# One bank for the first half's pooled maps, a first pair of merge gates and an earlier place for reloaded keys in an fp32 hybrid layer on one core

## The chip, the cores and the metric

The kernel runs as one program on one core of a Trainium2 chip. TensorE multiplies, VectorE (DVE in the profile), ScalarE (ACT) and GpSimd (POOL) do the rest, and SyncE (SP) starts most of the transfers. The metric is the time of one execution on the device in microseconds, the median of several.

## What is computed

One layer with two token mixers is applied to 2048 prompt rows and to 64 sample rows that continue a cached sequence of 4096 positions. All values are fp32.

```
h = rmsnorm(x);  q,k,v,ga,u,gb,mg = split(h @ w_in)        # 1024 columns each, mg 2048
att = stick_breaking(q, k, v)                              # 8 heads of 128; sample rows also see cache_k, cache_v
   A[t,s] = sigmoid(z_ts) * prod_{s<j<t} (1 - sigmoid(z_tj)),  s < t
pb  = (trailing_mean(u, 2|4|8|16) - u) per group of 256 columns, @ w_pool[group], * pool_scale
y_a = (att * silu(ga)) @ w_br_a;   y_b = (pb * silu(gb)) @ w_br_b
x   = x + (sigmoid(mg)[:, :1024] * y_a + sigmoid(mg)[:, 1024:] * y_b) @ w_out
return rmsnorm(x), k, v and the last 15 rows of u, for prompt and sample
```

## The kernel before

**Products.** Each fp32 operand is split into a high and a low part of reduced width (hi and lo in the names), and each product of 128 x 128 weights with up to 512 columns is three matmuls: hi with hi, lo with hi, hi with lo. A cast on ScalarE makes the high part and a subtraction on VectorE the low one; the function `split` issues both, and in the profile they appear in the lines of that helper (L91, L92, and L341 where program order is kept). So `wlo<-raw,whi` is the low part of a weight slab, `klo<-kback,khi` that of a block of keys that was read back from memory.

**Stages.** The rows are handled in two halves: the first has 1088 columns (1024 prompt rows and the 64 sample rows, in groups of 512, 256 and 320 in the profile), the second 1024. The stages follow each other in time, in us of the profiled execution:

- up to about 575: projections and attention of the first half, head by head;
- 575 to 1085: attention of the sample rows over the cache (`sample_stream`), with the first half's gates and its four pool groups (`rest`) between its steps;
- 1090 to 1790: projections and attention of the second half, some 93 us per head;
- 1795 to 1880: the attention left over from the last head, beside the branch gates (columns of `gb`) 0 to 3;
- 1880 to 2230: the second half's pool groups, branch gates 4 to 7 and the merge gates (the sixteen 128-column slabs of `mg`);
- then the branch products `w_br_a` and `w_br_b`, the merge, `w_out` (in steps n = 0 to 7) and the last norm.

**Order.** TensorE's instructions stand in the order in which the code issues them, over the whole program; `run((a, cost), (b, cost))` interleaves two generators by the nanoseconds that they yield. On ScalarE, VectorE and SyncE a scheduler sets the order in most of the program; inside `manual_schedule` blocks and in `placed_split` it is the code's order.

**Accumulators.** The eight PSUM banks are dealt out by name, two to each: `pj` for projections, `tr` for transposes and scans' tails, `att` for attention's output, `z` for scores. The sample attention keeps one `att` bank as its accumulator through a pair of heads.

**Pool groups.** `pool_group(half, gi)` projects two slabs of `u`, forms the trailing means and, in `mapped`, multiplies them with the 256 x 256 weights of the group: for each column group (g, of n columns), two products (s = 0 and 1, called A and B here), each of six matmuls into a PSUM tile, and then one multiplication on VectorE (L502, `gbl<-z,pscale,gbl`) that reads the tile and scales it with the gate. In the first half there are four groups with three column groups each, so 12 pairs A, B. In the groups of 512 columns the twelve matmuls of A and B stand back to back on TensorE; in those of 256 and 320 six projection matmuls stand between A and B.

**Second half's heads.** `Attention.scores(n)` is called for each of the 28 units of a head. Blocks of the first half's keys and values are read back from memory (`kback`, `vback`) and split at units that are set by a key: block cc of k at unit 5 - 2 cc, of v at 9 - 2 cc. A head's own late block of v (`late_v`, from the tile `nat`) is split at unit 1.

**Gates.** A slab of gates is eight chunks of weights times two groups of 512 columns, 48 matmuls (`proj`, lines 368 to 370). `proj_ahead` is `proj` with weights whose loads and splits were issued ahead by hooks in the attention units, from the list `cols_ahead`. Branch gates 6 and 7 (`branch_pair`) and merge gates 2 to 15 (`GATE_PAIRS`) are made two slabs at a time in seven products of 12 matmuls each, by a scheme of sums: the row sums of h (`hs["a11"]`, `hs["s1"]` and so on) are made once (`form_sums`), the sums of the weight blocks for each pair (`pair_forms`). Merge gates 0 and 1 are plain slabs of 48.

**The last stages.** `load_rows` fetches row blocks for the branch products, `weight_sums` forms the sums of `w_br` and `w_out` beside the merge gates, and `norm_sums` takes squares of the output rows on ScalarE (`bjk<-xo`, L1817) for the last norm.

## Time and profile before

| | |
|---|---|
| three runs | 2685.87, 2688.13, 2689.59 us; median 2688.13 |
| the profiled execution | 2687.25 us, of which the span of the core's instructions is 2685.5 |
| TensorE | busy 2663.5 us, 99% of the span, 15078 matmuls |
| VectorE | 1910.3 us, 71% |
| ScalarE | 1321.2 us, 49% |
| GpSimd | 418.4 us, 16% |
| memory | 341.40 MB moved by the queues, mean 127 GB/s |

A row of the timeline gives the start of an instruction in us after the start of the span, its duration, engine, line, operation, what it writes and reads, shapes, and in brackets how long its engine had been idle and what ended that. "x2" is two instructions in a row. The duration of a matmul contains its way through the array, so matmuls overlap: the pace is the distance of two starts. In the view of waits, a row gives the engine and line that waited, what ended the wait, the total in us, how often, and the longest.

### The profile page before, as it was taken

What the parts mean: (1) busy time and instruction counts of PE and PEld (TensorE: products, weight loads), DVE (VectorE), ACT (ScalarE), POOL (GpSimd) and SP (SyncE); (2) the same over time, 40 slices, a digit from 0 to 9 for tenths busy, and PEclk for the clock granted to TensorE, in tenths of its full rate; (3) what the DMA queues carried; (4) which work ended last, traced back from release to release, by engine and by line L of the source; (5) the groups of instructions that cost most, each with busy time, mean ns of one, the idle gap of its engine ahead of it and who ended that gap; (6) DMA issues with size and microseconds to landing.
All of it is one profiled execution on the core that took longest, in us unless ns stands there. A gap on an engine that the chain in (4) does not pass through costs nothing.

```text
span 2685.5 us, 42349 instructions
## 1 busy us (share of the span) xinstructions
PE 2663.5 (99%) x15078; PEld 2347.1 (87%) x15078; DVE 1910.3 (71%) x3016; ACT 1321.2 (49%) x2621; POOL 418.4 (16%) x1202
## 2 busy tenths in 40 slices
PE   9999999999999999999999999999999999999998
PEld 8999899988899989988888888888888889999886
DVE  6555555567777784488888888888956757677877
ACT  5446444455555553365556656655432443332443
POOL 1122222220000000021222222121001301111001
PEclk9999999999999999999999999999999999999999
DMA  5224222234444444222111111111345868787753
GB/s 152 82 82 131 75 74 74 80 100 151 154 150 154 153 151 159 83 59 59 44 48 57 58 36 60 56 40 48 118 134 169 281 204 290 234 283 252 257 176 118
DMA packets 336594, 341.40 MB, mean 127 GB/s; under 512 B 29736, under 2 KB 278944, under 8 KB 336383
## 3 DMA queue, kind: packets, MB, share of 16 engines
q1 hardware_dynamic: 322270, 292.82, 34.7%
q0 software_dynamic: 14112, 45.89, 4.7%
q8 instruction: 118, 1.93, 0.3%
q14 instruction: 94, 0.76, 0.1%
HBM read 229.97 MB, written 108.65 MB: 126 GB/s over the span
## 4 chain that ended last, share of the span: by engine, by line
PE 92%; DVE 5%; issue 1%; ACT 1%; POOL 1%; DMA 0%; DVEq 0%; POOLq 0%; SPq 0%; ACTq 0%
PE pj L368 15%; PE pj L369 15%; PE pj L370 15%; PE tr L819 4%; PE x L1528 3%; PE x L1532 3%; PE x L1530 3%; PE y L1532 3%; PE y L1528 3%; PE y L1530 2%; PE att L836 2%; PE att L835 2%; PE z L807 2%; PE att L834 2%; PE z L806 2%; PE z L805 2%
## 5 line engine op out<-in xcount | busy, mean ns | idle before, releaser
L368 PE MATMUL pj<-hhi,whi 128*128 128x512 f32 (+2 forms) x2320 | 830.2, 358 | 0.0
L370 PE MATMUL pj<-hhi,wlo 128*128 128x512 f32 (+2 forms) x2320 | 803.7, 346 | 0.0
L369 PE MATMUL pj<-hlo,whi 128*128 128x512 f32 (+2 forms) x2320 | 803.2, 346 | 0.3 <-DVE hlo L1072 0.3
L743 DVE TENSOR_TENSOR_SCAN om<-om 128x513 f32<-128x513 f32 (+3 forms) x356 | 387.0, 1087 | 193.4 <-POOL om L720 103.2
L370 PEld LDWEIGHTS pj<-hhi,wlo 128*128 128x128 f32 x2320 | 437.1, 188 | 52.0
L368 PEld LDWEIGHTS pj<-hhi,whi 128*128 128x128 f32 x2320 | 438.6, 189 | 46.9
L369 PEld LDWEIGHTS pj<-hlo,whi 128*128 128x128 f32 x2320 | 438.4, 189 | 45.3 <-DVE hlo L1072 0.5
L735 ACT ACTIVATE om<-z 128x512 f32<-128x512 f32 (+2 forms) x320 | 170.9, 534 | 291.1 <-PE z L807 270.1
L746 DVE TENSOR_TENSOR be<-be,om 128x512 f32<-128x512 f32 (+3 forms) x356 | 218.8, 614 | 33.4 <-ACT a L91 0.5
L92 DVE TENSOR_TENSOR a<-tr,a 128x512 fp32r<-128x512 f32 (+2 forms) x356 | 216.0, 607 | 28.2 <-ACT a L91 25.9
L91 ACT CAST a<-tr 128x512 fp32r<-128x512 f32 (+2 forms) x356 | 188.1, 528 | 86.5 <-PE tr L819 78.7
L745 POOL COPY carry<-om 128x1 f32<-128x1 f32 x356 | 71.6, 201 | 858.0 <-DVE om L743 832.0
L819 PE MATMUL tr<-ident,be 128*128 128x128 f32 x1088 | 173.9, 273 | 5.5 <-DVE be L746 4.4
L819 PEld LDWEIGHTS tr<-ident,be 128*128 128x128 f32 x1088 | 135.9, 140 | 38.9 <-DVE be L746 8.0
L736 ACT ACTIVATE be<-z 128x512 f32<-128x512 f32 (+2 forms) x320 | 169.5, 530 | 0.0
L92 DVE TENSOR_TENSOR wlo<-raw,whi 128x512 fp32r<-128x512 f32 x157 | 107.3, 688 | 84.5 <-ACT whi L91 83.9
L91 ACT CAST whi<-raw 128x512 fp32r<-128x512 f32 x160 | 98.7, 622 | 87.8 <-PE pj L369 76.6
L834 PE MATMUL att<-a,v 128*128 128x512 f32 (+1 forms) x320 | 132.7, 415 | 0.0
L836 PE MATMUL att<-a,v 128*128 128x512 f32 (+1 forms) x320 | 118.4, 370 | 1.8 <-DVE a L92 1.5
L807 PE MATMUL z<-khi,qlo 128*128 128x512 f32 (+2 forms) x320 | 117.0, 365 | 0.0
L835 PE MATMUL att<-a,v 128*128 128x512 f32 (+1 forms) x320 | 116.5, 364 | 0.0
L806 PE MATMUL z<-klo,qhi 128*128 128x512 f32 (+2 forms) x320 | 116.4, 364 | 0.0
(496 smaller groups left out, 5209.8 us busy)
## 6 DMA issues: line engine op xcount, KB each, us to landing
raw<-in_w_in_dram SPq DMA_DIRECT2D x228, 256.0 KB, 2.9
sg<-sm_d SPq DMA_DIRECT2D x48, 352.0 KB, 5.4
kraw<-in_cache_k_dram SPq DMA_DIRECT2D x64, 256.0 KB, 3.2
vraw<-in_cache_v_dram SPq DMA_DIRECT2D x64, 256.0 KB, 2.9
sm_d<-sgm SPq DMA_DIRECT2D x48, 256.0 KB, 3.0
wraw<-tw_d SPq DMA_DIRECT2D x22, 512.0 KB, 4.0
out_dram<-nat SPq DMA_DIRECT2D x42, 256.0 KB, 2.3
mp_d<-sg POOLq DMA_DIRECT2D x24, 352.0 KB, 5.1
```

The source lines that it names most:

```text
L91: nc.scalar.copy(hi, src)
L92: (nc.gpsimd if eng == "g" else nc.vector).tensor_tensor(lo, src, hi.bitcast(F32), op=ALU.subtract)
L368: nc.tensor.matmul(ps[:, 0:n], whi[:, k], hhi[:, k, c0:c0 + n], start=k == 0, stop=False)
L369: nc.tensor.matmul(ps[:, 0:n], whi[:, k], hlo[:, k, c0:c0 + n], start=False, stop=False)
L370: nc.tensor.matmul(ps[:, 0:n], wlo[:, k], hhi[:, k, c0:c0 + n], start=False, stop=k == KT - 1)
L735: nc.scalar.activation(om[:, off:512], z[:, off:512], AF.Sigmoid, scale=-SCALE)
L743: nc.vector.tensor_tensor_scan(rev, rev, rev, 1.0, op0=ALU.mult, op1=ALU.bypass)
L746: nc.vector.tensor_tensor(be[:, off:512], be[:, off:512], om[:, off + 1:513], op=ALU.mult)
L807: nc.tensor.matmul(z[:, off:512], qlo[:, qs], khi[:, 0:m], start=False, stop=True)
L819: nc.tensor.transpose(tr[:, i * P:(i + 1) * P], be[:, off + j * P:off + (j + 1) * P], ident)
L834: nc.tensor.matmul(self.acc[:, s], vhi[:, js], ahi[:, s], start=first, stop=False)
L836: nc.tensor.matmul(self.acc[:, s], vhi[:, js], alo[:, s], start=False, stop=last)
```

## The change

It has six parts.

1. In the first half, the pooled maps' PSUM tile is named `att` and not `z`. The order of TensorE's instructions stays as it was there.
2. In the second half's heads, reloaded blocks of keys are split at unit 3 - 2 cc, so cc = 1 at unit 1 and cc = 0 at unit 3; a late block of v at unit 2.
3. Branch gates 0 to 3 are no longer in `cols_ahead` and go through `proj`.
4. Merge gates 0 and 1 become a pair (`stream_forms`, `first_gates`) in seven products of 12 matmuls, behind the last pool group. Their weight sums and the first four of the pair 2, 3 (11 forms) are made by `stream_forms`, `pair_forms` makes the other three of that pair, and `weight_sums` takes its steps later.
5. Of `load_rows`, the blocks r12 and r22 are both fetched at step (5, 0).
6. `norm_sums(0)` of step n = 0 of `w_out` moves from the end of that step into step 1.

The order on TensorE at the first pooled maps of 512 columns, before and after (buffer numbers kept; a name with another number is another tile; "waits" names the engine whose semaphore is waited for). Rows of before:

```order
L500 MATMUL z_7660<-phi_7520,wplo_7343 128x512
L498 MATMUL z_7669<-phi_7428,wphi_7342 128x512
L499 MATMUL z_7669<-plo_7429,wphi_7342 128x512
L500 MATMUL z_7669<-phi_7428,wplo_7343 128x512
L498 MATMUL z_7669<-phi_7520,wphi_7342 128x512
L499 MATMUL z_7669<-plo_7521,wphi_7342 128x512
L500 MATMUL z_7669<-phi_7520,wplo_7343 128x512
L919 MATMUL z_7683<-khi_7451,q2_7106 128x512 [waits DVE_49]
```

The same place on TensorE now:

```order
L500 MATMUL att_7660<-phi_7520,wplo_7343 128x512
L498 MATMUL att_7669<-phi_7428,wphi_7342 128x512 [waits DVE_49]
L499 MATMUL att_7669<-plo_7429,wphi_7342 128x512
L500 MATMUL att_7669<-phi_7428,wplo_7343 128x512
L498 MATMUL att_7669<-phi_7520,wphi_7342 128x512
L499 MATMUL att_7669<-plo_7521,wphi_7342 128x512
L500 MATMUL att_7669<-phi_7520,wplo_7343 128x512
L918 MATMUL z_7683<-khi_7451,q2_7106 128x512
```

Nothing changed its place. The first matmul of B (tile 7669) now waits for VectorE, and the score product behind it no longer does: since the other `att` bank holds the sample attention's accumulator, A and B have the same bank.

On TensorE within the first merge gates, into which the last maps of the last pool group fall (`z<-phi`, set off behind their projections). Rows of before, where `pj<-hhi` is merge gate 0 as a plain slab:

```order
L498 MATMUL z<-phi,wphi 128x512
L499 MATMUL z<-plo,wphi 128x512
L500 MATMUL z<-phi,wplo 128x512
L368 MATMUL pj<-hhi,whi 128x512
L369 MATMUL pj<-hlo,whi 128x512
L370 MATMUL pj<-hhi,wlo 128x512
L368 MATMUL pj<-hhi,whi 128x512
L369 MATMUL pj<-hlo,whi 128x512
L370 MATMUL pj<-hhi,wlo 128x512
L514 MATMUL tr<-ident,hist 15x128 x2
L368 MATMUL pj<-hhi,whi 128x512
```

The same place now:

```order
L498 MATMUL z<-phi,wphi 128x512
L499 MATMUL z<-plo,wphi 128x512
L500 MATMUL z<-phi,wplo 128x512
L514 MATMUL tr<-ident,hist 15x128 x2
L1230 MATMUL pj<-s3hi,whi 128x512
L1231 MATMUL pj<-s3lo,whi 128x512
L1232 MATMUL pj<-s3hi,wlo 128x512
L1230 MATMUL pj<-s3hi,whi 128x512
```

Products with sums of h (`s3`) stand where plain slabs stood, and the list of TensorE's rows is 12 shorter (13498 for 13510); it differs nowhere else but in the names of part 1 and in line numbers.

On VectorE in the first units of the second half's second head (`om`, `be` and `a` are a unit's scan, weights and their low part). Rows of before:

```order
L341 TENSOR_TENSOR v<-nat,v 128x512
L743 SCALAR_TENSOR_TENSOR om<-om 128x257
L746 TENSOR_TENSOR be<-be,om 128x256
L92 TENSOR_TENSOR a<-tr,a 128x512
L341 TENSOR_TENSOR wlo<-raw,whi 128x512
L743 SCALAR_TENSOR_TENSOR om<-om 128x385
L746 TENSOR_TENSOR be<-be,om 128x384
L92 TENSOR_TENSOR a<-tr,a 128x512
L89 CAST khi<-kst 128x512
L92 TENSOR_TENSOR klo<-kst,khi 128x512
L341 TENSOR_TENSOR klo<-kback,khi 128x512
L743 SCALAR_TENSOR_TENSOR om<-om 128x513
```

The same place now, from one unit's start on:

```order
L341 TENSOR_TENSOR klo<-kback,khi 128x512
L742 SCALAR_TENSOR_TENSOR om<-om 128x257
L745 TENSOR_TENSOR be<-be,om 128x256
L92 TENSOR_TENSOR a<-tr,a 128x512
L341 TENSOR_TENSOR wlo<-raw,whi 128x512
L341 TENSOR_TENSOR v<-nat,v 128x512
L742 SCALAR_TENSOR_TENSOR om<-om 128x385
L745 TENSOR_TENSOR be<-be,om 128x384
L92 TENSOR_TENSOR a<-tr,a 128x512
L89 CAST khi<-kst 128x512
L92 TENSOR_TENSOR klo<-kst,khi 128x512
L341 TENSOR_TENSOR klo<-kback,khi 128x512
```

The block cc = 1 has moved up two units, to the front; the block cc = 0 has taken its place behind `klo<-kst`; and v stands one unit later, beside a weight's low part.

The diff, its core:

```
                 c = gi * 2 + s
-                pb = psum.tile([P, 512], F32, name="z")
+                pb = psum.tile([P, 512], F32, name="z" if half else "att")
                 co = slice(s * P, (s + 1) * P)
...
                     if late_v:
-                        placed.setdefault(hd, []).append((1, out["v"], c0h + c, vchunk, nat))
+                        placed.setdefault(hd, []).append((2, out["v"], c0h + c, vchunk, nat))
                     else:
...
                     cols_ahead.extend(o + h * P for h in range(1, H) for o in (OFF_K, OFF_V, OFF_Q, OFF_GA))
-                    cols_ahead.extend(OFF_GB + c * P for c in range(4))
             else:
...
                         nc.sync.dma_start(raw, kvd[kind, hd, cc])
-                        todo.append(({"k": 5, "v": 9}[kind] - 2 * cc, out[kind], cc, chunk, raw))
+                        todo.append(({"k": 3, "v": 9}[kind] - 2 * cc, out[kind], cc, chunk, raw))
                 todo.sort(key=lambda x: x[0])
...
         pns = slab_ns(1)
-        run((tail_att, tail_ns), (chain(*[proj_ahead(GROUPS_B, branch_gate(1, c)) for c in range(4)]), 4 * pns))
+        run((tail_att, tail_ns), (chain(*[proj(GROUPS_B, [branch_gate(1, c)]) for c in range(4)]), 4 * pns))
         settle(True)
...
+        def stream_forms(c0):
+            half = []
+            def put(src):
+                if not half:
+                    t = form_w()
+                    half.extend([x[:, 4 * h:4 * h + 4] for x in t] for h in range(2))
+                w = half.pop(0)
+                split(*w, src)
+                ready.append(w)
+            def part_raw(nm):
+                return late[0].tile([P, 512], F32, name=nm).rearrange("p (k c) -> p k c", k=4)
+            for c in (c0, c0 + 2):
+                b = {nm: raw_w(OFF_M + (c + j) * P, k) for nm, j, k in (("b11", 0, 0), ("b12", 1, 0), ("b21", 0, 4))}
+                b["b22"] = part_raw("r12")
+                col = OFF_M + (c + 1) * P
+                nc.sync.dma_start(b["b22"], win[:, col:col + P].rearrange("(k p) c -> p k c", p=P)[:, 4:8, :])
+                if c == c0:
+                    yield
+                put(b["b11"])
+                yield
+                put(b["b21"])
+                yield
+                t2 = part_raw("r11")
+                nc.vector.tensor_tensor(b["b11"], b["b12"], b["b11"], op=ALU.subtract)
+                nc.vector.tensor_tensor(t2, b["b22"], b["b11"], op=ALU.subtract)
+                put(t2)
+                yield
+                put(b["b11"])
+                yield
+                if c == c0:
+                    nc.vector.tensor_tensor(b["b12"], b["b22"], b["b12"], op=ALU.subtract)
+                    put(b["b12"])
+                    yield
+                    put(b["b22"])
+                    yield
+                    nc.vector.tensor_tensor(b["b21"], b["b21"], t2, op=ALU.subtract)
+                    put(b["b21"])
+        ready = []
+        def first_gates(c, prepare):
+            next(prepare)
+            next(prepare)
+            x = psum.tile([P, 512], F32, name="pj")
+            kept_x = {}
+            for p, nm in enumerate(("a11", "a12", "s2", "s1", "s3", "s4", "a22")):
+                if p in (1, 3):
+                    y = psum.tile([P, 512], F32, name="att")
+                acc = x if p in (0, 2, 4, 6) else y
+                gate_product(acc, ready.pop(0), hs[nm], p in (0, 1, 3))
+                if p in (0, 2, 3):
+                    kept_x[p] = late[0].tile([P, 512], F32, name=("r21", "r22", None, "r21")[p if p != 2 else 1])
+                    nc.scalar.copy(kept_x[p], acc)
+                elif p < 6:
+                    gate_sum(c + (p != 1), p == 4, acc, kept_x.pop({1: 0, 4: 3, 5: 2}[p]))
+                else:
+                    last_gate.append(lambda: gate_out(c, 1, acc))
+                for _ in range({1: 2, 3: 1, 5: 2}.get(p, 0)):
+                    next(prepare)
+                yield 12 * mm_ns(512)
+        last_gate = []
         def lead(prepare):
...
         run((pool_group(1, 2), 2 * pns), (lead(prepare), 1.0))
-        run((chain(branch_pair(6, prepare), pool_group(1, 3), proj(GROUPS_B, [merge_gate(1, 0)])), 1.0))
+        run((chain(branch_pair(6, prepare), pool_group(1, 3)), 1.0))
+        prepare = stream_forms(0)
+        next(prepare)
+        next(prepare)
+        next(prepare)
+        run((first_gates(0, prepare), 1.0))
         settle(True)
...
                 (b11, b12), (b21, b22) = [[t[:, :, j * P:(j + 1) * P] for j in range(2)] for t in raws.pop(c)]
-                yield pair_form(b11)
-                yield pair_form(b21)
+                kept_forms = c > GATE_PAIRS[0]
+                if kept_forms:
+                    yield pair_form(b11)
+                    yield pair_form(b21)
                 t2 = gw.tile([P, 4, P], F32, name="gt2")
                 nc.vector.tensor_tensor(t2, b22, b11, op=ALU.subtract)
-                yield pair_form(t2)
-                yield pair_form(b11)
+                if kept_forms:
+                    yield pair_form(t2)
+                    yield pair_form(b11)
                 nc.vector.tensor_tensor(b12, b22, b12, op=ALU.subtract)
...
         pair_loads(GATE_PAIRS[0])
+        last_gate.pop()()
         forms_of = pair_forms()
-        ready = []
-
-        def some_forms():
-            for _ in range(4):
-                yield 1.0
-                ready.append(next(forms_of))
-
-        run((chain(*[proj(GROUPS_B, [merge_gate(1, c)]) for c in range(1, GATE_PAIRS[0])]), 10.0), (some_forms(), 8.0))
         closing_sums = weight_sums()
...
                         gate_sum(c + (p != 1), p == 4, acc, kept_x.pop({1: 0, 4: 3, 5: 2}[p]))
+                    if c == GATE_PAIRS[0]:
+                        next(prepare, None)
                     w = next(forms_of, None)
                         ready.append(w)
-                    next(closing_sums, None)
+                    if c > GATE_PAIRS[0] or p > 2:
+                        next(closing_sums, None)
                     if c + 2 == GATE_PAIRS[1]:
...
                 weights_at(2 * s + cc)
-                if more and (p, cc) in ((2, 0), (3, 0), (5, 0), (5, 1)):
-                    load_rows(s + 7 - p, {2: "r11", 3: "r21", 5: ("r12", "r22")[cc]}[p])
+                if more and (p, cc) in ((2, 0), (3, 0), (5, 0)):
+                    for nm in {2: ("r11",), 3: ("r21",), 5: ("r12", "r22")}[p]:
+                        load_rows(s + 7 - p, nm)
                 if not more and (p, cc) == (5, 1):
...
             elif not last:
+                if n == 1:
+                    norm_sums(0)
                 norm_sums(1)
...
             product(x, of.pop((n, "a22")), wo["t4"], False, cols, whole)
-            if not last:
+            if n and not last:
                 norm_sums(0)
```

## The prediction

> **What bounds the kernel now.** I read the page first, its busy times, the granted clock and the chain that ended last:
>
> ```profile
> PE 2663.5 (99%) x15078; PEld 2347.1 (87%) x15078; DVE 1910.3 (71%) x3016; ACT 1321.2 (49%) x2621; POOL 418.4 (16%) x1202
> PEclk9999999999999999999999999999999999999999
> PE 92%; DVE 5%; issue 1%; ACT 1%; POOL 1%; DMA 0%; DVEq 0%; POOLq 0%; SPq 0%; ACTq 0%
> ```
>
> TensorE is busy for 99% of the span at full clock and carries 92% of the chain. So the time is the number of matmuls times their pace, plus the moments in which TensorE waits. Only two kinds of edit can move it: matmuls added or removed, and waits of TensorE made or ended. The second view is therefore the waits of TensorE over the whole span (its largest rows), the third the busy time by stretches of the stages that the change touches:
>
> ```profile
> PE tr L819 <- DVE be L746: 4.4, 10, 1.2
> PE z L919 <- DVE gbl L502: 1.9, 4, 0.7
> PE att L836 <- DVE a L92: 1.5, 3, 0.9
> ...
> 1795.00:1885.00 90.00, 87.32 (x437) 70.78 (x436) 74.87 (x101) 50.59 (x99) 18.34 (x58) 1.00 0.16 55
> 1885.00:2060.00 175.00, 175.00 (x778) 144.59 (x777) 123.39 (x221) 57.28 (x103) 4.46 (x8) 1.00 0.40 128
> ```
>
> There is little to win: four waits of 1.9 us in all are owed to the pooled maps' banks (L502 frees them), the tail of the second half's attention (1795 to 1885) holds 90 − 87.32 = 2.68 us of idle TensorE, and the gates behind it hold none. Last, the timeline at the places that the change touches. The pace of matmuls, and the cost of a wait:
>
> ```profile
> 626.12 0.40 PE L499 MATMUL z<-plo,wphi 128*128 128x512 f32 x1
> 626.36 0.40 PE L500 MATMUL z<-phi,wplo 128*128 128x512 f32 x1
> 627.28 0.40 PE L498 MATMUL z<-phi,wphi 128*128 128x512 f32 x1
> 627.48 0.75 DVE L502 SCALAR_TENSOR_TENSOR gbl<-z,pscale,gbl 128x512 f32<-128x512 f32 x1 [0.20 <-PE z L500]
> 628.87 0.75 DVE L502 SCALAR_TENSOR_TENSOR gbl<-z,pscale,gbl 128x512 f32<-128x512 f32 x1 [0.64 <-PE z L500]
> 629.68 0.50 PE L919 MATMUL z<-khi,q 128*128 128x512 f32 x1 [0.38 <-DVE gbl L502]
> ```
>
> From 626.12 to 627.28 are five starts, (627.28 − 626.12)/5 = 0.23 us each. A matmul's 0.40 reaches 0.17 past the next possible start, so an idle time in brackets understates the loss by 0.17. The score product at 629.68 starts 0.06 after the end of the scaling that it waited for (628.87 + 0.75 = 629.62): that is the price of a release.
>
> **The maps in one bank (part 1).** No instruction comes or goes. At 627.28 the product B starts without a wait while VectorE only begins to scale A (627.48). In the changed order B's first matmul waits for that scaling. So each of the 12 pairs costs the end of A's scaling, plus 0.06, less B's start of before, where this is positive. The other three pairs of 512 columns, B's start and then A's scaling:
>
> ```profile
> 746.07 0.39 PE L498 MATMUL z<-phi,wphi 128*128 128x512 f32 x1
> 747.22 1.41 DVE L502 SCALAR_TENSOR_TENSOR gbl<-z,pscale,gbl 128x512 f32<-128x512 f32 x2
> 864.78 0.40 PE L498 MATMUL z<-phi,wphi 128*128 128x512 f32 x1
> 866.32 0.74 DVE L502 SCALAR_TENSOR_TENSOR gbl<-z,pscale,gbl 128x512 f32<-128x512 f32 x1
> 982.50 0.40 PE L498 MATMUL z<-phi,wphi 128*128 128x512 f32 x1
> 983.84 0.75 DVE L502 SCALAR_TENSOR_TENSOR gbl<-z,pscale,gbl 128x512 f32<-128x512 f32 x1
> ```
>
> The first pair gives 628.23 + 0.06 − 627.28 = 1.01; with 0.75 for one scaling the others give 1.96, 2.34 and 2.15, because VectorE is behind with the sample attention there: 7.5 us. In the pairs of 256 and 320 columns six projection matmuls stand between A and B and cover part of it. Of the four pairs of 256 the first and the last, and the one pair of 320 in which the scaling is late:
>
> ```profile
> 635.80 0.28 PE L498 MATMUL z<-phi,wphi 128*128 128x256 f32 x1
> 637.20 0.48 DVE L502 SCALAR_TENSOR_TENSOR gbl<-z,pscale,gbl 128x256 f32<-128x256 f32 x1
> 992.25 0.28 PE L498 MATMUL z<-phi,wphi 128*128 128x256 f32 x1
> 992.81 0.48 DVE L502 SCALAR_TENSOR_TENSOR gbl<-z,pscale,gbl 128x256 f32<-128x256 f32 x1
> 888.88 0.31 PE L498 MATMUL z<-phi,wphi 128*128 128x320 f32 x1
> 889.38 0.55 DVE L502 SCALAR_TENSOR_TENSOR gbl<-z,pscale,gbl 128x320 f32<-128x320 f32 x1
> ```
>
> They give 1.94 and 1.10, the two between them, read the same way, about 0.5 and 2.2: 5.7. The pair of 320 gives 889.93 + 0.06 − 888.88 = 1.1, the other three nothing. Gross: 7.5 + 5.7 + 1.1 = 14.3 us. Against it the four waits of the scores for a z bank end, 1.9 + 4 × 0.17 = 2.6. Net **+11.7**. Behind the waiting matmul stand the rest of B, then a score product, whose result ScalarE copies for VectorE; those get it later by the same time, but they follow TensorE and catch up while it stands. Low end: VectorE is free each time, every pair of 512 costs the first one's 1.01, the others nothing, 4.0 − 2.6 = +1.4. High end: the waits for a bank come back elsewhere, and one operation more of VectorE, as long as the longest shown below (1.75), falls in front of a scaling: 14.3 + 1.8 = +16.1. I take the middle value since the order on VectorE ahead of each first scaling is the old one.
>
> **The pair of merge gates (part 4).** 7 × 12 = 84 matmuls for 2 × 48 = 96: 12 × 0.23 = **−2.8**. The forms take the places of the weights' splits on VectorE, which has room there; first row, the low part of merge gate 0, second, the next form after both gates, before which VectorE lay idle for 10.76 us:
>
> ```profile
> 2022.98 0.69 DVE L92 TENSOR_TENSOR wlo<-raw,whi 128x512 fp32r<-128x512 f32 x1 [0.16 <-ACT whi L91]
> 2054.46 0.69 DVE L92 TENSOR_TENSOR flo<-graw,fhi 128x512 fp32r<-128x512 f32 x1 [10.76 <-ACT fhi L91]
> ```
>
> Eleven forms and their differences are some 17 operations of 0.69, 12 us over the pair's 20: hidden. Without that cover, a form that waits for its weights would stop TensorE for the length of a transfer and a split; I bound that by 3 us. Ends −2.8 and +0.2.
>
> **Keys and values at other units (part 2).** The waits in the second half's heads are one per head; the first, the second and the last:
>
> ```profile
> 1154.29 0.30 PE L819 MATMUL tr<-ident,be 128*128 128x128 f32 x1 [0.78 <-DVE a L92]
> 1238.40 0.33 PE L819 MATMUL tr<-ident,be 128*128 128x128 f32 x1 [0.47 <-DVE be L746]
> 1704.88 0.33 PE L819 MATMUL tr<-ident,be 128*128 128x128 f32 x1 [0.44 <-DVE be L746]
> ```
>
> The first goes (0.78 + 0.17). The six of later heads stay: they follow the jam of `klo<-kst` and `klo<-kback`, and the block cc = 0 now lands where cc = 1 stood. New is v beside a weight's low part one unit earlier, 0.69 more on VectorE in one unit. I take **−0.6**; ends −4.5 (all seven gone, 0.95 + 6 × 0.6) and +2 (0.3 in each head).
>
> **The tail of attention, and plain branch gates (parts 2 and 3).** Its waits, and what VectorE and GpSimd do just before:
>
> ```profile
> 1799.46 1.59 DVE L341 TENSOR_TENSOR klo<-kback,khi 128x512 fp32r<-128x512 f32 x1
> 1799.22 1.29 POOL L840 TENSOR_TENSOR ao<-ao,sga 128x512 f32<-128x512 f32 x1
> 1804.12 0.44 PE L836 MATMUL att<-a,v 128*128 128x384 f32 x1 [0.29 <-DVE a L92]
> 1809.37 0.33 PE L819 MATMUL tr<-ident,be 128*128 128x128 f32 x1 [1.24 <-DVE be L746]
> 1851.11 1.75 DVE L341 TENSOR_TENSOR wlo<-raw,whi 128x512 fp32r<-128x512 f32 x1
> 1855.66 0.44 PE L836 MATMUL att<-a,v 128*128 128x384 f32 x1 [0.94 <-DVE a L92]
> ```
>
> The two subtractions take 1.59 and 1.75 where their like take 0.69 (rows above), the first beside GpSimd's product, and each is followed by waits. Now the keys' one comes four units sooner, and the weights' low parts of the branch gates are made by `proj`, which feeds branch gates 4 and 5 behind with no idle TensorE (175.00 of 175 above). All of it is 2.68 + 4 × 0.17 = 3.4; some subtractions stay in the tail, so I take two thirds, **−2.3**, ends −3.4 and 0. The Trainium skill, page "SBUF — State Buffer", section "Who interferes with whom", says that a VectorE instruction with two SBUF inputs contends with a GpSimd instruction that reads SBUF; the trace agrees here (1.59 against 0.69), and by that rule alone the term would be the two stretches, 0.90 + 1.06 = 2.0.
>
> **The rest (parts 5 and 6).** The squares of step n = 0 stand ahead of the copy of x on ScalarE, for which TensorE waits once:
>
> ```profile
> 2539.00 0.50 PE L1528 MATMUL x<-t2hi,rhi 128*128 128x512 f32 x1 [0.59 <-ACT x L1543]
> ```
>
> In step 1 they stand behind such a copy: 0.59 + 0.17 = **−0.8**, ends −0.8 and +0.8 (they delay the next copy). Row loads and later weight sums cost nothing: VectorE's 10.76 us of idle and the gates between them and the branch products hide them; without these they would stop TensorE for a transfer, as a late form would (3 us).
>
> **Sum.** +11.7 − 2.8 − 0.6 − 2.3 − 0.8 = **+5.2 us**. The profiled execution took 2687.25, which gives 2692.4; the median of the runs is 0.88 higher, and on it the sum is 2693.3, +0.19%. What a measurement can tell from no change is about 0.2%, 5.4 us (2682.7 to 2693.5), so the forecast lies at that edge.
>
> **Rivals.** (a) VectorE is free when the first maps end, and the one bank costs only its low end: 1.4 − 6.5 = −5.1, 2683.0, faster from a little better on. For it speaks the first pair, where VectorE idled 0.20 us before the scaling; against it the pairs at 635, 746, 864 and 982, in which the scaling began 1.15 to 1.54 us after B's old start. The place to look is the six waits at 635, 746, 864, 877, 982 and 992; it decides where they sum to less than 5 us. (b) The waits pile up: the scores' bank waits come back and the gains of the tail and the keys stay out, 5.2 + 2.6 + 2.9 = +10.7, 2698.8. For it speaks that VectorE is also late elsewhere (the 4.4 us of the first waits row), against it that the removed waits have no other cause in the order. (c) The pair's forms come late by 3 us at its first or third product: 2696.3. (d) The maps don't share a bank and part 1 only removes the waits: −2.6 − 6.5 = −9.1, 2679.0; the wait in the changed order speaks against it. (e) The nine new stalls slow the clock: half pace for 12 matmuls after each is 9 × 12 × 0.23 = 25 us, 2718. Against it, the granted clock is 1.00 in the stretch from 1795 to 1885 with its 2.68 us of waits. The Trainium skill, page "TensorE: Matmul & The Clock Gate", section "A second HAM failure mode: psum-queue depth-cycling", tells of a kernel in which short idle times between groups of matmuls let the clock swing to half; the rows here do not show that for stalls up to 1.24 us.
>
> **How the numbers follow.** The sum as it stands has 0.62; its own range is 2689 to 2697 (the bank's net by ±3, the other terms by ±2), 0.36 within 0.2% and 0.26 above. (a) 0.13, half faster and half the same; (b) 0.15, slower; (c) 0.06, mostly slower; (d) 0.03, faster; (e) 0.01. Faster 0.10, same 0.44, slower 0.46. The range from 2685 to 2699 takes in the sum's own range, (b), (c) and the upper part of (a).
>
> **What would show it.** Right: waits of TensorE for L502 at the maps of about 14 us, half of it at the four pairs of 512 columns, no wait of the scores for L502, 12 matmuls fewer with no wait from 2030 to 2055, the waits near 1809 and 1855 gone, the one at 2539 gone, those near 1238 to 1705 still there. Wrong: VectorE's scaling of A begins right behind A's last matmul (then the time falls to the left end), or waits of over 0.3 us in the heads' second unit or at the pair (right end).

## The result, and the profile after

The changed kernel takes 2708.57 us (median of four runs, 2708.32 to 2711.49) beside 2687.73 us of the kernel before (its median over four runs): the ratio is 1.0077, with an interval from 1.0065 to 1.0090. It is slower by 20.8 us where 5.2 were forecast, and outside the range. Of all runs told below two took far longer, 5359.67 us (the kernel before, beside e1 to e4) and 7021.77 us (e9); they count in the medians and not in the ratios. The profiled execution of the changed kernel has a span of 2706.5 us against 2685.5. Of the page the span and the row of the engines:

```profile
span 2706.5 us, 42389 instructions
PE 2670.0 (99%) x15066; PEld 2350.8 (87%) x15066; DVE 1916.2 (71%) x3028; ACT 1327.7 (49%) x2627; POOL 419.0 (15%) x1202
```

TensorE has 12 matmuls fewer (15066 for 15078) and is nevertheless busy for 6.5 us longer: part of the loss is not waiting but slower matmuls. The largest rows of its waits over the span:

```profile
PE att L498 <- DVE gbl L502: 12.9, 9, 2.2
PE tr L818 <- DVE be L745: 6.4, 11, 1.5
PE z L1230 <- ACT gx L1419: 3.0, 1, 3.0
...
PE y L1600 <- DVE rlo L92: 0.6, 1, 0.6
PE att L1230 <- ACT whi L91: 0.5, 1, 0.5
```

The first row is the one bank of the maps: nine waits, as read from before. The third and the fifth of the rows shown are new and were not forecast: they lie at the first pair that the kernel before made in seven products too, merge gates 2 and 3. The waits of the scores for L502 and the wait at 2539 are gone. Since the order on TensorE is known, the same matmul can be found in both traces, and the difference of its starts shows where the time went:

| stretch of before, us | shift gained there, us | what it is made of |
|---|---|---|
| 0 to 575 | −0.2 | |
| 575 to 1085, maps and sample attention | +15.4 | nine waits +14.4, four ended −2.6, slow matmuls +3.2, slower starts after releases +0.4 |
| 1085 to 1795, heads | +0.5 | first head −0.6, the others +1.1 |
| 1795 to 1885, tail | −0.2 | |
| 2031 to 2058, merge gates 0 and 1 | −2.7 | 12 matmuls |
| 2058 to 2070, merge gates 2 and 3 | +5.7 | waits 0.6 and 3.2, restarts 0.3, slow matmuls 1.6 |
| 2200 to 2225, first branch products | +0.9 | a wait for `rlo` |
| 2225 to 2537, branch products and w_out | +2.0 | pace of the 352-column matmuls |
| 2537 to 2685 | −0.3 | −0.9 at the old wait, +0.6 after it |

The slow matmuls are seen in the busy time by stretches (TensorE's busy time and matmuls, the granted clock, then the transfers). Four stretches of 3.4 us, each right behind a wait, of 2.18, 2.35, 2.02 and 3.16 us from start to start:

```profile
638.00:641.40 3.40, 3.23 (x17) 0.63 0.71 220
874.00:877.40 3.40, 3.40 (x14) 0.56 0.26 98
889.50:892.90 3.40, 3.37 (x22) 1.00 0.49 154
2083.20:2086.60 3.40, 3.40 (x9) 0.56 0.82 255
```

Behind three of the four the granted clock is 0.56 to 0.63 of full over the 3.4 us, and in the last nine matmuls stand where 15 fit at 0.23 us. This is the half clock that the prediction had put at 1 in 100.

The waits at merge gates 2 and 3, in rows picked from the timeline of ScalarE, with the two matmuls of TensorE that waited and GpSimd's issue of the weight sums' loads (`ws`) among them:

```profile
2071.07 0.59 ACT L1419 COPY gx<-z 128x512 f32<-128x512 f32 x1 [2.11 <-PE z L1232]
2071.07 2.35 POOL L1429 DMA_DIRECT2D ws<-in_w_br_a_dram  x4 [171.77 <-PE z L1232]
2076.24 0.62 ACT L91 CAST whi<-raw 128x512 fp32r<-128x512 f32 x1 [4.58 <-PE z L1231]
2076.91 0.50 PE L1230 MATMUL att<-s1hi,whi 128*128 128x512 f32 x1 [0.48 <-ACT whi L91]
2079.55 0.62 ACT L91 CAST fhi<-graw 128x512 fp32r<-128x512 f32 x1 [2.69 <-DVE graw L1411]
2081.53 0.63 ACT L1222 ACTIVATE sgm<-gx 128x512 f32<-128x512 f32 x1 [1.36 <-DVE gx L1235]
2082.57 0.58 ACT L1419 COPY gx<-z 128x512 f32<-128x512 f32 x1
2083.20 0.80 PE L1230 MATMUL z<-s3hi,fhi 128*128 128x512 f32 x1 [3.00 <-ACT gx L1419]
```

The eleventh form's cast (2076.24) stands on ScalarE behind the copy of the first product, but starts only when TensorE has finished the third product, 4.58 us later: it waits for a weight buffer. TensorE's fourth product needs this form (0.48). Behind the cast stand, in order, the next forms and the copy of the third product (2082.57), and the fifth product writes into the bank that this copy frees: 3.00 us. The loads of the weight sums, issued at 2071.07, use buffers of the same two tags as the forms, and had taken the one that the first product freed.

### The profile page after: what moved, and what is told of

Same layout as the page of the kernel before. It is cut to its first block, busy times and chain, and to the rows that moved or that the text cites. A ratio compares the mean times of both kernels' runs of the same rounds, so it can differ in the third digit from the quotient of the medians.

```text
span 2706.5 us, 42389 instructions
## 1 busy us (share of the span) xinstructions
PE 2670.0 (99%) x15066; PEld 2350.8 (87%) x15066; DVE 1916.2 (71%) x3028; ACT 1327.7 (49%) x2627; POOL 419.0 (15%) x1202
## 3 DMA queue, kind: packets, MB, share of 16 engines
q8 instruction: 118, 1.93, 0.3%
## 4 chain that ended last, share of the span: by engine, by line
PE 87%; DVE 7%; issue 3%; ACT 1%; DMA 1%; POOL 1%; POOLq 0%; SPq 0%; DVEq 0%; ACTq 0%
PE pj L368 14%; PE pj L369 14%; PE pj L370 14%; PE tr L818 4%; PE x L1598 3%; PE x L1602 3%; PE x L1600 3%; PE y L1602 2%; PE y L1600 2%; PE y L1598 2%; DVE om L742 2%; PE att L835 2%; PE z L806 2%; PE att L834 2%; PE z L805 2%
## 5 line engine op out<-in xcount | busy, mean ns | idle before, releaser
L368 PE MATMUL pj<-hhi,whi 128*128 128x256 f32 (+2 forms) x2288 | 818.3, 358 | 0.0
L369 PE MATMUL pj<-hlo,whi 128*128 128x256 f32 (+2 forms) x2288 | 791.5, 346 | 0.3 <-DVE hlo L1071 0.3
L370 PE MATMUL pj<-hhi,wlo 128*128 128x256 f32 (+2 forms) x2288 | 791.8, 346 | 0.0
L92 DVE TENSOR_TENSOR wlo<-raw,whi 128x512 fp32r<-128x512 f32 x169 | 115.6, 688 | 98.6 <-ACT whi L91 98.0
L91 ACT CAST whi<-raw 128x512 fp32r<-128x512 f32 x172 | 106.4, 622 | 99.0 <-PE pj L369 77.0
```

Source lines behind the costliest of these rows:

```text
L91: nc.scalar.copy(hi, src)
L92: (nc.gpsimd if eng == "g" else nc.vector).tensor_tensor(lo, src, hi.bitcast(F32), op=ALU.subtract)
L368: nc.tensor.matmul(ps[:, 0:n], whi[:, k], hhi[:, k, c0:c0 + n], start=k == 0, stop=False)
L369: nc.tensor.matmul(ps[:, 0:n], whi[:, k], hlo[:, k, c0:c0 + n], start=False, stop=False)
L370: nc.tensor.matmul(ps[:, 0:n], wlo[:, k], hhi[:, k, c0:c0 + n], start=False, stop=k == KT - 1)
```

## Experiments

All of these leave the computation whole. Their ratios are to runs of the kernel before on the same chip, whose medians were 2688.94 (e1 to e4), 2687.72 (e5 to e7) and 2688.07 us (e8, e9).

**The change without its first part (e1), and the first part alone (e2).**

```
 e1, in the changed kernel           e2, in the kernel before
-name="z" if half else "att"        -name="z"
+name="z"                           +name="z" if half else "att"
```

> The changed kernel with its first part undone: the first half's maps are in the z banks again, all else as changed. Theory: the stretch from 575 to 1085 us gave 15.5 of the 21 us (11.8 of net waits for the scaling, 3.7 of matmuls at half clock behind two of them), so the time falls by about 15.5 to 2693, the four waits of the scores come back, and no stretch near 640 or 875 has a granted clock below 0.95. Rival: the slow matmuls near 640 and 875 belong to the place (weights or transfers there), not to the stalls: then the fall is 11.8, to 2697, and they stay slow.

> The kernel before with the first part alone (maps in the att banks). Theory: +15.5 us, about 2703, with nine waits of 14.4 us together for the scaling and at least one stretch at half clock behind a wait of over 2 us. Rival, the waits alone cost: +11.8, about 2699.5.

e1 took 2689.23 us, ratio 1.0003 (0.9994 to 1.0013); e2 2703.04 us, ratio 1.0056 (1.0041 to 1.0071). So most of the loss is the first part, and without it the rest of the change is worth nothing in sum. The times do not simply add up: the first part costs 14.1 us alone and 20.5 on top of the rest (20.8 against 0.3). The traces differ there by falls of the clock (one more near 638 and one at the merge gates, some 1.5 us each) and by the pace of the last stage, but one trace of each kernel cannot say how often either comes. The stretch from 575 to 1085 is −15.5 us in e1 beside the changed kernel, as expected, with the scores' four waits back (first row); 0.4 of it is lost again before 575. Two things were not expected: the wait of 3.0 us at merge gates 2 and 3 is there in e1 too, but this time without a fall of the clock (rows two and three), which is 1.3 us less there, and the last stage runs 2.0 us faster. With 0.5 less at the first branch products the spans differ by 18.8 and not 15.5.

```profile
PE z L918 <- DVE gbl L502: 1.9, 4, 0.7
...
2068.12 0.50 PE L1230 MATMUL z<-s3hi,fhi 128*128 128x512 f32 x1 [3.00 <-ACT gx L1419]
2068.10:2071.50 3.40, 3.38 (x15) 1.00 0.74 227
```

In e2 the nine waits are the same, but only one of the two waits that were followed by slow matmuls in the changed kernel is so here:

```profile
PE att L498 <- DVE gbl L502: 12.8, 9, 2.2
...
638.70:642.10 3.40, 3.36 (x24) 1.00 0.67 210
872.50:875.90 3.40, 3.40 (x14) 0.69 0.20 77
```

The same instruction with the same wait (2.18 us) was followed by half clock in one execution and by full clock in the other. It is therefore not the place alone. The runs of e2 spread from 2700.3 to 2705.9.

**What decides on the clock (p1, p2).** Ahead of the second half's pool groups of the kernel before stand 60 batches of matmuls with a stall of known length between them; nothing else is changed. The edit in short, not word for word:

```
+ for i in range(60):
+     for j in range(n):  matmul(ps, wt if j == 0 else hhi[:, j % 8, 0:P], hhi[:, j % 8, 512:1024], ...)
+     tensor_tensor(t2, ps, t); further operations of VectorE on t2, about 0.3*(i % 12) us   # p2: 0.55 + 0.1*(i % 10)
+     wt = t2[:, 0:P] - t2[:, 0:P]          # the next batch's first weights
```

> The kernel before with a probe ahead of the second half's pool groups: 60 batches of 52 to 82 matmuls of 512 columns, and behind each a chain of VectorE operations on which the next batch's first matmul depends, so that TensorE stands for about 0.9 to 4.2 us in twelve steps of 0.3, five of each at different distances. Only the trace counts. Theory (the clock falls when TensorE has been idle for the larger part of some window of time whose position is not tied to the kernel): no slow matmuls behind stalls below 1.5 us, in some cases behind those of 2 to 3, in all behind those over 3.5, at half pace for a fixed time of some 3.4 us, 1.7 us lost each. Rival (the slow matmuls depend on what is stalled, the maps or the gates): full pace behind all of them.

> The same probe with stalls between about 1.5 and 2.8 us in ten steps of some 0.1, six of each, behind batches of other lengths. Only the trace counts. In the first probe none of ten stalls up to 1.72 us was followed by slow matmuls, one of five at 1.98, four of five at 2.44 and all five at 2.70. Theory (a window of time not tied to the kernel decides): the share of stalls with slow matmuls rises step by step from none near 1.8 to all near 2.6, with both outcomes at one and the same length. Rival (a fixed length of idle time decides): one length below which none and above which all are followed by them.

In p1 none of the ten stalls up to 1.72 us (from start to start, less the pace) was followed by slow matmuls, one of five at 1.98, four of five at 2.44, all ten at 2.70 and 3.16, four of five at 3.42, and all 24 above 3.8. In p2 both outcomes came at every length from 1.94 to 3.12 but 3.03 and a single stall of 2.04, and the share did not rise steadily: two of five at 1.94, five of six at 2.49, one of six at 2.66, all six at 3.03, one of five at 3.12. Two stalls of one length from p1, each with the stretch behind it, and two from p2:

```profile
2408.46 0.50 PE L1193 MATMUL z<-hhi,pw 128*128 128x512 f32 x1 [1.83 <-DVE pw L1202]
2408.50:2411.50 3.00, 3.00 (x13) 1.00 0.00 0
2884.44 0.50 PE L1193 MATMUL z<-hhi,pw 128*128 128x512 f32 x1 [1.83 <-DVE pw L1202]
2884.50:2887.50 3.00, 3.00 (x9) 0.64 0.00 0
```

```profile
2595.43 0.50 PE L1193 MATMUL z<-hhi,pw 128*128 128x512 f32 x1 [2.96 <-DVE pw L1202]
2595.50:2598.50 3.00, 3.00 (x13) 1.00 0.00 0
2397.87 0.50 PE L1193 MATMUL z<-hhi,pw 128*128 128x512 f32 x1 [2.96 <-DVE pw L1202]
2397.90:2400.90 3.00, 3.00 (x10) 0.73 0.02 5
```

A fixed length of idle time does not decide. What fits is a window: if time is cut into pieces of 3.413 us with one starting point for each execution, "more than some 1.9 us idle within one piece" tells the stalls with slow matmuls from those without, for all 59 stalls of p1 and all 59 of p2. (The length was looked for from 1.6 to 1.8 and from 3.38 to 3.44 us.)

That fit is a calculation on the rows, but the granted clock in the traces shows the pieces themselves. All 43 falls of p1 and all 33 of p2 are stretches at half clock of 3.41 us or of twice that, and within one execution their starts lie on a grid of 3.413 us, to within 0.001 us. With this grid in place of a fitted starting point (its pieces ended 0.1 us before the recorded falls, which fits best) 116 of the 118 stalls come out right at 1.93 us. The three falls of the changed kernel, at 638.91, 874.43 and 2082.75, lie 69 and then 354 such pieces apart. The first, with the piece before it and the piece behind it:

```profile
635.49:638.91 3.42, 1.40 (x11) 1.00 0.27 79
638.91:642.32 3.41, 3.41 (x16) 0.50 0.48 154
642.32:645.73 3.41, 3.41 (x18) 1.00 0.67 210
```

This also answers for the two waits that were followed by half clock in one execution and not in the other. The wait of 2.18 us near 638 lies in one piece in the changed kernel; in e2 the grid of its one fall (873.76) parts it into 1.69 and 0.50. Of the 3.16 us at merge gates 2 and 3, 2.72 lie in one piece in the changed kernel; in e1 the grid, counted back from the half clock behind its last matmuls (2684.38), parts them into 1.62 and 1.55. The two pieces of e1:

```profile
2063.16:2066.57 3.41, 1.96 (x9) 1.00 0.13 47
2066.57:2069.98 3.41, 1.86 (x8) 1.00 0.81 214
```

The Trainium skill, page "TensorE: Matmul & The Clock Gate", section "Part 1: The HAM clock gate", describes such a free-running window of 3413 ns; the probes agree with its length and its free phase. It puts the fall behind a whole idle window, and here the measurement decides otherwise: somewhat over half a window is enough. The price in the probes is 1.3 to 1.6 us, 6 to 9 matmuls at 0.43 us in place of 0.23, for the 60 falls of one piece; the 16 of two pieces cost 1.7 to 2.9, and all but three of them stand behind stalls above 3.8 us.

**A bank for each map (e3).** In the kernel before:

```
-pb = psum.tile([P, 512], F32, name="z")
+pb = psum.tile([P, 512], F32, name="att" if s and not half else "z")
```

> The kernel before, with A's maps in a z bank and B's in the free att bank, so that each has a bank of its own and a score product finds the other z bank free. Theory: no wait for the scaling at B and none at the scores but where A's bank is the next in turn: between -1.5 and -2.6 us, about 2685.5. Rival: the scores' waits were not for the bank but for VectorE's own lateness and come back at the next product that reads its results: no change.

e3 took 2685.08 us, ratio 0.9992 (0.9982 to 1.0001). In its trace from 575 to 1085 one wait is left that has nothing to do with the maps, and the shift over the stretch is −2.8, of which −2.6 are the whole price of the scores' four waits:

```profile
PE tr L819 <- DVE be L746: 0.3, 1, 0.3
```

So the waits for a z bank can be had for nothing, with the spare att bank for B alone. The comparison of times by itself does not part it from no change, and the profiled execution lost more than that elsewhere: 0.5 before 575, 2.0 by the pace of the last stages (below) and 1.4 behind 2500, most of it in one wait for `sg` that no other of these traces has.

**The weight sums' loads behind the eleventh form (e4).** In the changed kernel:

```
 closing_sums = weight_sums()
-next(closing_sums)
 ...
                     if c == GATE_PAIRS[0]:
                         next(prepare, None)
+                        if p == 0:
+                            next(closing_sums)
```

> The changed kernel, with the first loads of the weight sums issued behind the first product of the pair 2, 3, so that they take the buffers behind the eleventh form and not ahead of it. Theory: the cast of the eleventh form waited for the buffer of the tenth, since the loads had taken the ninth's; ScalarE's copies and sums stood behind it in order. Then the waits at 2076 and 2080 (0.6 and 3.0 us) and the half clock behind them go: -5.5 us, about 2703. Rival: the forms are late because their weights arrive late (the four loads of that pair landed 4 to 10 us after their issue): then the 3.0 us stay and at most 0.8 is won.

e4 took 2702.79 us (1.0056, 1.0041 to 1.0071), 5.8 less than the changed kernel, and TensorE has no wait from 2030 to 2100. The cast now follows the copy at once, though no weights arrive sooner for it: the last load of `raw` landed at 2061.05 us in the changed kernel and at 2061.37 in e4, the pair's loads of `graw` at 2071.89 and 2073.62 against 2071.87 and 2073.77.

```profile
2071.27 0.59 ACT L1419 COPY gx<-z 128x512 f32<-128x512 f32 x1 [2.12 <-PE z L1232]
2071.75 0.62 ACT L91 CAST whi<-raw 128x512 fp32r<-128x512 f32 x1
```

That shows the buffer as the cause; late weights, the rival, are excluded for this wait.

**Both mends together, and single parts undone from there (e5 to e9).** e5 is the changed kernel with the edits of e3 and e4; e6 is e5 with part 2 undone, e7 e5 with part 3 undone, e8 e6 with part 5 undone, e9 e6 with the weight sums' steps begun two products sooner.

```
 e6, on e5:  {"k": 3, "v": 9} -> {"k": 5, "v": 9};  placed late v: 2 -> 1
 e7, on e5:  proj(...) -> proj_ahead(...) for branch gates 0 to 3, and their columns in cols_ahead again
 e8, on e6:  r12 at step (5, 0), r22 at step (5, 1)
 e9, on e6:  if c > GATE_PAIRS[0] or p > 2  ->  p > 0
```

> The changed kernel with the two mends together: A's maps in z and B's in att, and the first loads of the weight sums behind the eleventh form. Theory: of the change remain -2.3 (scores' waits), -2.7 (12 matmuls), and the small terms of the trace, +0.9 in the heads, -0.7 in the tail, +0.4 at the first branch product, -0.2 at the norm: -4.6, about 2684.3 beside 2688.9. Rival: what TensorE doesn't wait for here it waits for at the next edge: 2688.

> As the kernel with the two mends, and the second part undone (keys at units 5 and 3, late v at unit 1). Theory: the later units made each later head's wait 0.15 to 0.3 us longer and ended the first head's; undone, the heads between 1085 and 1795 lose 0.9 less and the first wait of 0.8 returns: -0.5 in all, and the tail's keys are late again there, +0.5 to +1: about 2684.5. Rival: the longer waits of the heads come from the scheduler's other order of the weights' low parts, not from the units: then the heads keep +0.9.

> As the kernel with the two mends, and the third part undone (branch gates 0 to 3 formed ahead by hooks). Theory: the tail's waits come from VectorE's jam with keys and weights; with the weights ahead again the tail loses 0.5 to 1 us more than with proj, about 2685. Rival: the weights ahead are what keeps the tail's other waits away, and the tail gains: about 2683.5.

e5 took 2683.60 us (0.9982, 0.9973 to 0.9991), e6 2682.42 us (0.9974, 0.9964 to 0.9983), e7 2683.40 us (0.9982, 0.9973 to 0.9992). The times do not part these three; their traces do. The waits of the heads (1085 to 1800) of the kernel before, of e5 and of e6, a fence each:

```profile
PE tr L819 <- DVE be L746: 2.5, 6, 0.5
PE tr L819 <- DVE a L92: 0.8, 1, 0.8
```

```profile
PE tr L818 <- DVE be L745: 3.7, 6, 0.8
PE tr L818 <- DVE a L92: 0.3, 1, 0.3
```

```profile
PE tr L818 <- DVE be L745: 2.7, 6, 0.5
PE tr L818 <- DVE a L92: 0.8, 1, 0.8
```

Part 2 shortens the first head's wait by 0.5 and lengthens the six later ones by 1.2; undone, both go back, but for 0.2 of the 1.2. In the tail (1795 to 1885) the shift against the kernel before is −0.2 in e5, −0.2 in e6 and −0.3 in e7, where e6 and e7 were each expected to move it by 0.5 to 1 us: with either part alone the tail takes as long as with both.

> As the kernel with the two mends and keys back, and the fifth part undone (row block r22 fetched at step (5, 1) again). Theory: the wait of 0.7 us at the first branch product comes from the weight sums' transfers, which end later than before, not from these loads: no change beside 2682.4. Rival: the loads of both blocks at one step crowd the queue: -0.7.

> As the kernel with the two mends and keys back, and the weight sums take up their steps two products sooner within the pair 2, 3. Theory: their sums reach memory sooner, the first weights for the branch products land before TensorE needs them, and the wait at the first branch product (0.7 us) goes: -0.5 to -0.7, about 2681.8. Rival: the sums stand ahead of the pair's last forms on VectorE and stop TensorE there: +1 or more.

e8 took 2682.94 us (0.9978, 0.9968 to 0.9987), no different from e6, as expected. e9 took 2685.17 us (0.9984, 0.9975 to 0.9994) and went the rival's way: a wait at merge gates 2 and 3, 1.4 us from start to start and 1.8 in the shift of the gates,

```profile
PE z L1230 <- DVE gx L1235: 1.1, 1, 1.1
```

and the wait at the first branch products did not go (1.0). That wait does not hang on the later parts alone: it stands in the profiled execution of e2 as well (1.0), which has none of them, and not in that of e4, which has all of them (0.3 in the shift). Whether they make it more frequent is open: it stands in seven of eight traces with them and in one of three without.

The lowest median is that of e6, the changed kernel with both mends and the keys where they were: 5.3 us below the kernel before. The times of e5, e7 and e8 do not part from it.

## Why the prediction was wrong, step by step

The sum was +5.2 and the profiled execution is 21.0 us longer. Of the 15.8 us between them 4.8 are matmuls at half clock, 4.2 the waits at merge gates 2 and 3, 2.1 the tail, 2.0 the pace of the last stage, 1.1 the heads, 0.9 the first branch products, 0.5 the norm squares; the small rest is the bank and the start. So the sum failed in the main where it put two things at nothing: what a long wait does to the clock, and what a new form on ScalarE holds up.

**The bank (forecast +11.7): right in size and place.** Gross 14.3 us was forecast and the nine waits cost 14.4 from start to start; the four ended ones gave 2.6 back. The places were those named. What the step left out is that a matmul behind a long wait may run at half clock.

**The clock, rival (e), chance 0.01: with the pair's waits the main failure.** The rival was refused because the granted clock was 1.00 in a stretch with waits up to 1.24 us, while the waits that the same text had just worked out reach 2.35 us. A row says nothing about a wait twice as long as any it holds; the longest wait anywhere in before was 1.6 us. The rival's own price was wrong as well (25 us for half pace behind all nine). Two of the nine waits and the one at merge gates 2 and 3 were followed by it, 1.6 us each, 4.8 in all. Which waits are hit is chance: it hangs on where the pieces of 3.413 us lie in an execution, and no row of before could tell that.

**The pair (forecast −2.8): its matmuls right, its surroundings not.** The gates 0 and 1 gave −2.7 with no wait. The failing sentence is that the forms are hidden because VectorE has room. VectorE had room; what was not looked at is ScalarE's order and the buffers. The eleventh form is a new instruction ahead of copies that TensorE waits for, and its buffer had been given to the weight sums' loads. The rival (c) of late forms had the right kind but stood at the wrong pair, with 3 us and 0.06; it cost 5.7, 1.6 of it by the clock. e4 shows that the buffer was the cause.

**Keys and values (−0.6): the sign was wrong, +0.5.** The first head gained 0.6 as forecast. The six later waits were said to stay; they grew, by 0.1 to 0.3 each. That v beside a weight's low part costs something was in the range (0.3 in each head) but not in the sum; e6 shows that part 2 is the cause, not which of its two moves.

**The tail (−2.3): −0.2.** The two stretched subtractions were taken for the cause of the waits behind them because they came before them. Two waits did end, the one of `att` near 1804 (−0.5) and the one near 1855 (−1.0), but the largest, at 1809.37 before, grew from 1.24 to 1.51, and longer delays elsewhere, 0.4 of them at one new wait, took back the rest. The keys' subtraction left the tail and takes 0.68 us where it stands now, so the stretch itself went as forecast, but it was not what TensorE waited for. Nor was VectorE behind with its work: some 5 us before the largest wait ended it lay idle for 1.51 us (by accident the same number). VectorE in the changed kernel, and the matmul that waited (rows left out at the dots):

```profile
1819.84 1.23 DVE L742 TENSOR_TENSOR_SCAN om<-om 128x513 f32<-128x513 f32 x1 [1.51 <-ACT om L734]
...
1822.71 1.22 DVE L742 TENSOR_TENSOR_SCAN om<-om 128x513 f32<-128x513 f32 x1
1823.85 0.67 DVE L341 TENSOR_TENSOR v<-vback,v 128x512 fp32r<-128x512 f32 x1
1824.43 0.69 DVE L745 TENSOR_TENSOR be<-be,om 128x512 f32<-128x512 f32 x1
1825.18 0.33 PE L818 MATMUL tr<-ident,be 128*128 128x128 f32 x1 [1.51 <-DVE be L745]
```

Before, a gate's product stood in the place of this `v<-vback`, between the scan (`om`) and its weights (`be`). That an operation at this place makes the wait, and any other would do the same, is argued, not tested.

**The norm squares (−0.8): −0.3.** The old wait gave 0.9, of which 0.6 came back behind it, within the ends given.

**Not in the sum at all:** the wait at the first branch products (+0.9, which by e2 can come without the later parts and by e4 can stay away with them) and the last stage's pace (+2.0, below).

## What to carry to other kernels

A wait that a change adds must be held against the longest wait that the profile shows: beyond that its price is not only its length, and here a wait above some 1.9 us could cost 1.3 to 1.6 us more. When new instructions are put on an engine that lies idle, look at the buffers they take and at what stands behind them in order; the idle time of the engine says nothing of either. And before two users are put on one buffer, give the spare one to one of them: here half of the edit (B alone in the att bank) had all of its gain and none of its cost.

## What the hardware showed unexpectedly

The half clock behind stalls of 1.94 us and more has been told with the probes. The other observation is the pace of the matmuls of 352 columns in the last stages, which differs between executions. Busy time and matmuls of TensorE from 2260 to 2500 in the kernel before and in the changed one, no waits in either:

```profile
2260.00:2500.00 240.00, 240.00 (x1503) 1.00 0.78 260
```

```profile
2260.00:2500.00 240.00, 240.00 (x1492) 1.00 0.76 258
```

That is a mean of 160.0 ns before and 161.1 ns after; in e1 and e7 it was 160.0, in e3, e4 and e6 161.1, in e2, e5, e8 and e9 158.9. Over the roughly 2000 such matmuls a nanosecond is 2 us, so the three paces lie 4 us apart, somewhat less than half of the spread between runs of one kernel (2685.07 to 2694.55 for the kernel before, beside e5 to e7). It follows no edit of these programs; the cause stays open, and one profile of each kernel cannot tell a program's own pace from an execution's.
